# A two-block transformer kernel: the modulation's weight rows get three half-size slots of their own

## The chip, the core and the metric

One core of one Trainium2 chip runs the whole program. The metric is device time in microseconds (us) of one execution; a measurement is the median of several. A kernel is one launch, and everything it reads lies in the device's memory at the start.

## What is computed

Two model blocks over 256 tokens of width 2048, in float32, and between them a normalisation. The first block holds a state-space branch (s5), a delta-rule branch and a convolved feed-forward net of width 5632; the second holds windowed attention, an RWKV branch and a second feed-forward net. The change concerns the second block's modulation, twelve shifts, scales and gates that come from a vector `c` (and from `c_ctx`) alone:

```python
mod = jax.nn.silu(c) @ ada_w + ada_b          # ada_w: 2048 x 12288
mod_c = jax.nn.silu(c_ctx) @ ada_w + ada_b
sh1, sc1, g1, sh2, sc2, g2 = jnp.split(mod[:, None, :], 6, axis=-1)
sh1c, sc1c, g1c, sh2c, sc2c, g2c = jnp.split(mod_c, 6, axis=-1)
z = modulate(rmsnorm_2(x, norm1_g), sh1, sc1) @ w_in
zc = modulate(rmsnorm_2(xc, norm1_g), sh1c, sc1c) @ w_in
```

Nothing of it depends on the first block, so it can be computed at any time before it is used: `sh1`, `sc1` of both vectors before the second block's norms, `g1`, `sh2`, `sc2` before the attention's output is added, `g2` at the very end.

## The kernel before

**The dense layers.** Nearly all of the time goes into matrix products with large weights, written once in `dense`. It walks over a weight matrix in chunks of 256 rows by 512 columns, 928 of them. For each chunk `wchunk` loads 512 KB into a tile `w` (L233, on SyncE's queue, SP), ScalarE rounds it to fp32r into `wr` (L236), VectorE subtracts to get the rest `wl` (L237), and TensorE does 24 matmuls: weights `wr` with the high and the low part of the activations (L265, L266) and `wl` with the high part (L268). There are two slots each for `wr` and `wl` and four for `w`, and each slot is used again in turn.

**The modulation.** A matrix with one row of activations is poor work for TensorE, so VectorE does it: `ada_rows` copies a quarter of the activated vector into a PSUM tile on all partitions (`ada_c`, L197), loads weight rows of the transposed matrix, and multiplies and sums 512 columns of 128 outputs with one SCALAR_TENSOR_TENSOR and its accumulator read (L209) into a column of `part`. One such multiplication is called a step below. 512 steps are needed: 32 groups of 128 outputs for each of the two vectors (`ada_start`, 256 steps), 48 more for `c` (`ada_next`, 192 steps), and the last 16 (`ada_last`, 64 steps). A load brings two steps (512 KB, L191) into a tile `w_ada` that takes one of the same four slots as the weights' `w`, and is issued one load ahead of its use.

**What sets the order.** `ada_rows` is a generator. `dense` adds `tick_rate` after every chunk and takes one tick of the generator for each whole one (L269 to L273); the rate is 0.7, 0.3, 0.75, 0.27 and 0.25 in turn (in `program` and `ada_last`). This gives the order of the text. The order in which the five engines and the DMA queue get their instructions is then set by a scheduler that plays the program through with estimated times (`schedule_with_timeline_sim=True`): an instruction of a later place in the text can come earlier on its engine if its inputs and its slot are free. So what limits how early a step can come is, above all, when its tile's slot comes free. On the chip each engine, and SP's queue, works strictly in the order it was given.

**Places that the text speaks of.** `s5` (L879) works in eight groups, on VectorE for the most part (tiles that the profile calls s_p, s_v, s_f, s_r; each group ends with `s_y`, L928), beside the gate layers' chunks; `s5_out` splits its result into `ys5h` and `ys5l`, which the layer `glu` needs, followed by `w_out1`. `ffn1` is the first feed-forward net, whose evacuation on VectorE is a convolution (`fconv`, L1074). `rw_out` (L1519) finishes the RWKV branch head pair by head pair (tiles xr, rw_nsq, and the split `rwh`, `rwl`), which the second half of the layer `w_out2` needs. `ffn2` is the last net.

Of the kernel before, what the change touches and what calls it, by code (L numbers as in the profile page):

```python
# [10 lines left out]
F32 = mybir.dt.float32  # L11
# [3 lines left out]
ALU = mybir.AluOpType  # L15
# [61 lines left out]
class Feat:  # L77


    def __init__(self, tiles):  # L80
        self.tiles = tiles
# [8 lines left out]
class Kern:  # L90
    def __init__(self, ctx, tc, a):
        self.ctx, self.tc, self.nc, self.a = ctx, tc, tc.nc, a
        mk = lambda n, b, **k: ctx.enter_context(tc.tile_pool(name=n, bufs=b, **k))
        self.pc = mk("const", 1)
        self.pw = mk("w", 3)
        self.pb = mk("b", 1)
        self.ps = mk("ps", 1, space=PSUM)
        self.pd = mk("dr", 1, space=DRAM)
        self.n = 0
        self.ada = None  # L100
        self.N4, self.NQ, self.N2, self.NE, self.N1, self.NW, self.NWR, self.NWL = 20, 11, 8, 5, 5, 4, 2, 2


    def feat(self, n, name, dt=F32):
# [46 lines left out]
    def setup(self):  # L151
        nc, tc = self.nc, self.tc
        self.pv = self.pc.tile([128, NPV], F32, name="pv")
        nc.gpsimd.dma_start(self.pv, self.a["pv"])
        self.cst = self.pc.tile([128, NCS], F32, name="cst")
        nc.gpsimd.dma_start(self.cst, self.a["cst"])
        self.ones = self.pc.tile([128, 128], F32, name="ones")
        nc.vector.memset(self.ones, 1.0)
        self.eps = {}
        for nm, v in (("e6", EPS), ("e12", EPS * EPS), ("e6x128", 128 * EPS), ("lnx", 64e-5), ("hpi", float(np.pi / 2))):  # L160
            t = self.pc.tile([128, 1], F32, name="eps_" + nm)
            nc.vector.memset(t, v)
            self.eps[nm] = t

        th = self.t1([128, 32], name="c_th")
        o = PV["c"][0]
        cc = self.pv[:, o:o + 32]
        nc.scalar.activation(th, cc, AF.Tanh, scale=0.5)
        nc.vector.scalar_tensor_tensor(cc, th, 1.0, cc, ALU.add, ALU.mult)
        nc.vector.tensor_scalar(cc, cc, 0.5, None, ALU.mult)  # L170
        self.sil = cc
        self.part = self.pc.tile([128, 48, 4], F32, name="part")
        self.mod = self.pc.tile([128, 2, 96], F32, name="mod")


# [2 lines left out]

    def ada_next(self):
        self.ada_end()  # L180
        self.ada = self.ada_rows(0, 32, 80)

    def ada_rows(self, which, n0, n1, wide=2):

        nc = self.nc
        W = self.a["ada_wT"].rearrange("(n p) k -> p n k", p=128)
        nxt = None

        def load(q, n):
            w = self.pw.tile([128, 2, 512], F32, tag="w", name="w_ada", bufs=self.NW)  # L190
            nc.sync.dma_start(w, W[:, n:n + wide, q * 512:q * 512 + 512])  # L191
            return w
        for q in range(4):
            ps = self.ps.tile([128, 512], F32, tag="ada", name="ada_c", bufs=1)
            for j in range(4):
                k = which * 16 + q * 4 + j
                nc.tensor.matmul(ps[:, j * 128:j * 128 + 128], lhsT=self.sil[:, k:k + 1].to_broadcast([128, 128]),  # L197
                                 rhs=self.C("ident"), start=j == 0, stop=j == 3)
            for n in range(n0, n1, wide):

                if nxt is None:
                    nxt = load(q, n)
                w, nxt = nxt, None
                if n + wide < n1:
                    nxt = load(q, n + wide)
                elif q < 3:
                    nxt = load(q + 1, n0)
                for i in range(wide):
                    nc.vector.scalar_tensor_tensor(w[:, i], w[:, i], 1.0, ps, ALU.mult, ALU.mult,  # L209
                                                   accum_out=self.part[:, n - n0 + i, q:q + 1])  # L210
                yield n
        m = self.mod[:, which, n0:n1]
        nc.vector.reduce_sum(m, self.part[:, :n1 - n0], axis=mybir.AxisListType.X)
        nc.vector.tensor_tensor(m, m, self.P("ada_b")[:, n0:n1], ALU.add)
# [4 lines left out]

    def ada_last(self):  # L220
        self.ada_end()
        self.tick_rate = 0.25
        self.ada = self.ada_rows(0, 80, 96)

    def ada_tick(self):
# [50 lines left out]


    ticks = 0.0
    tick_rate = 0.7

    def split(self, hh, ll, src):

# [1469 lines left out]
    def program(self, out):  # L1752
# [5 lines left out]
        self.z_gate()  # L1758
        self.u_proj()
        self.dn_out()  # L1760
        self.tick_rate = 0.3
        self.s5_setup()
        self.s5()
        self.dn_proj()
        self.gs_gate()
        self.s5_out()
        self.tick_rate = 0.75
        self.glu()
        self.w_out1()
        self.ada_next()  # L1770
        self.tick_rate = 0.27
        self.mod1()
        self.rw_setup()
        self.ctx_path()
# [125 lines left out]
```

## Time and profile before

| | |
|---|---|
| time of three runs, median (lowest to highest) | 3565.49 us (3563.25 to 3572.38) |
| the profiled execution, its own time | 3570.66 us |
| its span, first to last instruction | 3568.9 us |
| TensorE matmul (PE), weight load (PEld) | busy 93%, 86% |
| VectorE (DVE), ScalarE (ACT), GpSimd (POOL) | busy 72%, 42%, 0% |
| mean granted TensorE clock | 0.961 of full speed |
| DMA | 635.13 MB, mean 178 GB/s |

The span is the profiled execution seen by its instructions; the time beside it has what lies around them. The trace is of one execution, so its numbers are compared with that execution's own 3570.66 us. Busy shares are means over stretches that are limited by different engines; the clock column (PEclk) is the share of full speed that TensorE was granted, and since its two levels are 1.2 and 2.4 GHz, a mean between 0.5 and 1 tells how long it was at the lower one.

### The profile page before, as it was taken

To read this page: it belongs to the slowest core of one execution; us is meant where nothing else is said; L and a number is where in the kernel's file an instruction comes from. 1 tells how busy PE (TensorE), PEld (TensorE's weight loads), DVE (VectorE), ACT (ScalarE), POOL (GpSimd) and SP (SyncE) were. 2 spreads that over 40 slices of the span, in tenths; PEclk is the share of its full clock that TensorE was granted. 3 is DMA by queue.
4 is the path that set the end of the run, shared out by engine and by line. 5 is a ranking of instruction groups with operands and counts; after the bars stand their busy time and mean duration, and the time that the engine had idled before them with its cause. 6 is when DMAs were issued, how large, how long until landed. Compare 5 with 4: busy or idle time off the path is not lost. (4 is left out here: it accounts for less than half of the span.)

```text
span 3568.9 us, 72631 instructions
## 1 busy us (share of the span) xinstructions
PE 3322.8 (93%) x30516; PEld 3086.5 (86%) x30516; DVE 2577.8 (72%) x4497; ACT 1515.1 (42%) x2148; POOL 16.9 (0%) x46
## 2 busy tenths in 40 slices
PE   7889999978999999999999998997899999999998
PEld 6778888857899898899999988886687999999998
DVE  7778899876768788866666778586765666655556
ACT  4443444424445444443344444444443443333333
POOL 0000000000000000000000000000000000000000
PEclk9889999979999999999999999998899999999999
DMA  7665566548776454456666656341022666765554
GB/s 244 205 216 183 167 182 196 181 139 277 239 224 190 135 166 154 155 175 198 211 203 217 212 181 190 111 141 63 19 92 84 200 222 230 228 195 184 183 184 142
DMA packets 342408, 635.13 MB, mean 178 GB/s; under 512 B 22112, under 2 KB 46432, under 8 KB 342080
## 3 DMA queue, kind: packets, MB, share of 16 engines
q1 hardware_dynamic: 341856, 629.42, 55.5%
q8 instruction: 239, 3.92, 0.4%
q0 software_dynamic: 224, 1.07, 0.1%
q14 instruction: 89, 0.73, 0.1%
HBM read 625.17 MB, written 4.72 MB: 176 GB/s over the span
## 5 line engine op out<-in xcount | busy, mean ns | idle before, releaser
L236 ACT CAST wr<-w 128x1024 fp32r<-128x1024 f32 (+2 forms) x928 | 953.4, 1028 | 1418.9 <-PE acc L266 1144.0
L237 DVE TENSOR_TENSOR wl<-w,wr 128x1024 fp32r<-128x1024 f32 (+2 forms) x928 | 1108.8, 1197 | 526.0 <-ACT wr L236 487.1
L265 PE MATMUL acc<-hh,wr 128*128 128x256 f32 (+2 forms) x4976 | 1266.6, 289 | 46.2 <-DVE conv L345 13.4
L266 PE MATMUL acc<-hl,wr 128*128 128x256 f32 (+2 forms) x4976 | 1260.4, 288 | 1.8 <-DVE hl L284 1.5
L265 PEld LDWEIGHTS acc<-hh,wr 128*128 128x128 f32 (+2 forms) x4976 | 970.1, 195 | 69.1 <-issue 28.1
L266 PEld LDWEIGHTS acc<-hl,wr 128*128 128x128 f32 (+2 forms) x4976 | 970.7, 195 | 14.0 <-issue 9.4
L268 PE MATMUL acc<-hh,wl 128*128 128x256 f32 (+2 forms) x4976 | 761.5, 289 | 40.3 <-DVE wl L237 39.8
L268 PEld LDWEIGHTS acc<-hh,wl 128*128 128x128 f32 (+2 forms) x4976 | 667.4, 195 | 69.1 <-DVE wl L237 50.0
L209 DVE SCALAR_TENSOR_TENSOR w_ada<-w_ada,ada_c 128x512 f32<-128x512 f32 x512 | 331.8, 683 | 216.6 <-DMA w_ada<-in_ada_wT_dram 213.0
L265 PE MATMUL acc<-hid,wr 128*128 128x256 f32 x1408 | 357.2, 287 | 4.8 <-DVE fconv L1074 3.2
L266 PE MATMUL acc<-hid,wr 128*128 128x256 f32 x1408 | 353.6, 284 | 0.0
L265 PEld LDWEIGHTS acc<-hid,wr 128*128 128x128 f32 x1408 | 271.4, 193 | 9.2 <-issue 5.0
L266 PEld LDWEIGHTS acc<-hid,wr 128*128 128x128 f32 x1408 | 271.5, 193 | 1.1 <-issue 1.0
L268 PE MATMUL acc<-hid,wl 128*128 128x256 f32 x1408 | 224.3, 286 | 4.7 <-DVE wl L237 4.6
L268 PEld LDWEIGHTS acc<-hid,wl 128*128 128x128 f32 x1408 | 191.9, 192 | 9.6 <-DVE wl L237 6.0
L1074 DVE SCALAR_TENSOR_TENSOR fconv<-acc,pv,fconv 128x255 f32<-128x255 f32 (+1 forms) x176 | 80.9, 477 | 8.8 <-ACT fconv L1072 7.6
L265 PE MATMUL acc<-ys5h,wr 128*128 128x256 f32 x256 | 66.6, 296 | 8.8 <-ACT wr L236 4.5
L265 PE MATMUL acc<-mrgh,wr 128*128 128x256 f32 x256 | 65.5, 292 | 6.0 <-ACT wr L236 5.9
L266 PE MATMUL acc<-ys5l,wr 128*128 128x256 f32 x256 | 65.7, 291 | 2.2 <-DVE ys5l L284 2.2
L1072 ACT ACTIVATE fconv<-acc,pv 128x256 f32<-128x256 f32 x88 | 40.6, 470 | 62.0 <-PE acc L268 33.2
L266 PE MATMUL acc<-mrgl,wr 128*128 128x256 f32 x256 | 64.3, 287 | 0.0
L265 PEld LDWEIGHTS acc<-ys5h,wr 128*128 128x128 f32 x256 | 50.7, 199 | 12.5 <-ACT wr L236 5.9
(532 smaller groups left out, 3679.4 us busy)
## 6 DMA issues: line engine op xcount, KB each, us to landing
w<-in_w_dram SPq DMA_DIRECT2D x264, 512.0 KB, 3.7
w<-in_w_in_dram SPq DMA_DIRECT2D x256, 512.0 KB, 4.2
w_ada<-in_ada_wT_dram SPq DMA_DIRECT2D x256, 512.0 KB, 4.3
w<-in_ffn_up_dram SPq DMA_DIRECT2D x176, 512.0 KB, 4.2
w<-in_ffn_down_dram SPq DMA_DIRECT2D x88, 512.0 KB, 4.1
w<-in_w_out_dram SPq DMA_DIRECT2D x64, 512.0 KB, 4.3
w<-in_glu_w_dram SPq DMA_DIRECT2D x32, 512.0 KB, 4.8
w<-in_dn_proj_dram SPq DMA_DIRECT2D x16, 512.0 KB, 3.7
```

Of the source, the lines that this page charges most:

```text
L209: nc.vector.scalar_tensor_tensor(w[:, i], w[:, i], 1.0, ps, ALU.mult, ALU.mult, accum_out=self.part[:, n - n0 + i, q:q + 1])
L236: nc.scalar.copy(r[:, :kb, :w], t[:, :kb, :w])
L237: nc.vector.tensor_tensor(l[:, :kb, :w], t[:, :kb, :w], r[:, :kb, :w].bitcast(F32), ALU.subtract)
L265: nc.tensor.matmul(o, lhsT=a, rhs=xh(kt), start=kt == 0 and first_j, stop=False)
L266: nc.tensor.matmul(o, lhsT=a, rhs=xl(kt), start=False, stop=False)
L268: nc.tensor.matmul(o, lhsT=a, rhs=xh(kt), start=False, stop=kt == KT - 1 and last_j)
L1072: nc.scalar.activation(t[:, j], ps[:, j], AF.Copy, scale=w(2))
L1074: v.scalar_tensor_tensor(t[:, j, k:], ps[:, j, :256 - k], w(2 - k), t[:, j, k:], ALU.mult, ALU.add)
```

## The change

The modulation's tiles get a set of slots of their own (tag `wa`): three tiles of 512 columns, 256 KB of data each, so that a load brings one step instead of two. Loads are issued two steps ahead. The weights' tag `w` goes from four slots to three, which only weights use. Since a tick is now one step, every rate is doubled; `ada_next`'s 48 groups are done as 32 and 16, so that `part` needs 32 columns instead of 48, and the tile of ones becomes one column that is read as a broadcast.

```diff
-        self.N4, self.NQ, self.N2, self.NE, self.N1, self.NW, self.NWR, self.NWL = 20, 11, 8, 5, 5, 4, 2, 2
+        self.N4, self.NQ, self.N2, self.NE, self.N1, self.NW, self.NWR, self.NWL = 20, 11, 8, 5, 5, 3, 2, 2
...
-        self.ones = self.pc.tile([128, 128], F32, name="ones")
-        nc.vector.memset(self.ones, 1.0)
+        one = self.pc.tile([128, 1], F32, name="one")
+        nc.vector.memset(one, 1.0)
+        self.ones = one.to_broadcast([128, 128])
...
-        self.part = self.pc.tile([128, 48, 4], F32, name="part")
+        self.part = self.pc.tile([128, 32, 4], F32, name="part")
...
-        self.ada = self.ada_rows(0, 32, 80)
+        self.ada = itertools.chain(self.ada_rows(0, 32, 64), self.ada_rows(0, 64, 80))
...
         def load(q, n):
-            w = self.pw.tile([128, 2, 512], F32, tag="w", name="w_ada", bufs=self.NW)
-            nc.sync.dma_start(w, W[:, n:n + wide, q * 512:q * 512 + 512])
-            return w
...
+            w = self.pw.tile([128, 512], F32, tag="wa", name="w_ada", bufs=3)
+            nc.sync.dma_start(w, W[:, n, q * 512:q * 512 + 512])
+            ahead.append(w)
+        for i, (q, n) in enumerate(steps):
...
+            for st in steps[:2] if i == 0 else []:
+                load(*st)
+            if i + 2 < len(steps):
+                load(*steps[i + 2])
+            w = ahead.pop(0)
+            nc.vector.scalar_tensor_tensor(w, w, 1.0, ps, ALU.mult, ALU.mult, accum_out=self.part[:, n - n0, q:q + 1])
+            yield n
...
-        self.tick_rate = 0.25
+        self.tick_rate = 0.5
...
-    tick_rate = 0.7
+    tick_rate = 1.4
...
-        self.tick_rate = 0.3
+        self.tick_rate = 0.6
...
-        self.tick_rate = 0.75
+        self.tick_rate = 1.5
...
-        self.tick_rate = 0.27
+        self.tick_rate = 0.54
```

How the scheduler orders the engines with it is told below for VectorE at three places. Line numbers behind `ones` differ by one or two between the two kernels. Counted over the whole order, the steps that stand on VectorE ahead of the last split of s5's result (`ys5l`) are 184 before and 328 now; from the fourth `s_y` to that split they are 26 before and 80 now. The first 448 steps are done before the 592nd of the 928 weight chunks before, and before the 272nd now; the last 64 lie between the chunks 664 and 800 before, and between 640 and 672 now. Ahead of the last split of `rw_out` stand 448 before and 499 now.

VectorE, the last group but one of s5, before (s_p, s_v, s_f and s_r are s5's tiles, s_pw its product from TensorE):

```order
L914 TENSOR_TENSOR s_p_4795<-s_pw,s_r 128x512
L915 TENSOR_TENSOR s_p_4795<-s_pw,s_f 128x512
L914 TENSOR_TENSOR s_p_4805<-s_pw,s_r 128x512
L915 TENSOR_TENSOR s_p_4805<-s_pw,s_f 128x512
L916 TENSOR_TENSOR s_p_4795<-s_p_4795 128x256
L917 TENSOR_TENSOR s_p_4795<-s_p_4795 128x256
L916 TENSOR_TENSOR s_p_4805<-s_p_4805 128x256
L917 TENSOR_TENSOR s_p_4805<-s_p_4805 128x256
L921 SCALAR_TENSOR_TENSOR s_v<-s_mag,s_p_4795 128x256 x2
L921 SCALAR_TENSOR_TENSOR s_v<-s_mag,s_p_4805 128x256 x2
```

and a group of the same kind there with the change:

```order
L912 TENSOR_TENSOR s_p_4880<-s_pw,s_r 128x512
L913 TENSOR_TENSOR s_p_4880<-s_pw,s_f 128x512
L912 TENSOR_TENSOR s_p_4890<-s_pw,s_r 128x512
L913 TENSOR_TENSOR s_p_4890<-s_pw,s_f 128x512
L208 SCALAR_TENSOR_TENSOR w_ada,part<-w_ada,ada_c 128x512
L914 TENSOR_TENSOR s_p_4880<-s_p_4880 128x256
L915 TENSOR_TENSOR s_p_4880<-s_p_4880 128x256
L208 SCALAR_TENSOR_TENSOR w_ada,part<-w_ada,ada_c 128x512 x2
L914 TENSOR_TENSOR s_p_4890<-s_p_4890 128x256
L915 TENSOR_TENSOR s_p_4890<-s_p_4890 128x256
L919 SCALAR_TENSOR_TENSOR s_v<-s_mag,s_p_4880 128x256 x2
L208 SCALAR_TENSOR_TENSOR w_ada,part<-w_ada,ada_c 128x512
```

Steps that stood far behind, in `ffn1`, now stand between s5's operations.

VectorE in `ffn1`, where the convolution of a layer's result begins, before:

```order
L237 TENSOR_TENSOR wl<-w,wr 128x1024 x4
L209 SCALAR_TENSOR_TENSOR w_ada,part<-w_ada,ada_c 128x512 x2
L1074 SCALAR_TENSOR_TENSOR fconv<-acc_18127,pv,fconv 128x255
L1074 SCALAR_TENSOR_TENSOR fconv<-acc_18127,pv,fconv 128x254
L237 TENSOR_TENSOR wl<-w,wr 128x1024
```

and the same convolution with the change:

```order
L235 TENSOR_TENSOR wl<-w,wr 128x1024 x8
L1072 SCALAR_TENSOR_TENSOR fconv<-acc_18483,pv,fconv 128x255
L1072 SCALAR_TENSOR_TENSOR fconv<-acc_18483,pv,fconv 128x254
L235 TENSOR_TENSOR wl<-w,wr 128x1024
L1072 SCALAR_TENSOR_TENSOR fconv<-acc_18484,pv,fconv 128x255
```

No step stands in `ffn1` any more.

VectorE at the end of the RWKV branch, with the change (xr is the branch's result, rw_mean, rw_rs and rw_nsq belong to its normalisation, rw_S and rw_X to the recurrence); before, the same place has no step:

```order
L1531 SCALAR_TENSOR_TENSOR xr_24059<-rw_mean,xr_24059 128x256
L208 SCALAR_TENSOR_TENSOR w_ada,part<-w_ada,ada_c 128x512 x3
L1423 TENSOR_TENSOR rw_S<-rw_S,rw_pS 128x256
L1531 SCALAR_TENSOR_TENSOR xr_24059<-rw_mean,xr_24059 128x256
L1424 TENSOR_TENSOR rw_S<-rw_S,rw_el 128x256
L208 SCALAR_TENSOR_TENSOR w_ada,part<-w_ada,ada_c 128x512 x2
L1401 TENSOR_TENSOR rw_X<-rw_px,rw_P_29141 128x256
L208 SCALAR_TENSOR_TENSOR w_ada,part<-w_ada,ada_c 128x512
L382 RECIPROCAL rw_nsq<-rw_nsq 64x256
```

The steps of `ada_last`, which stood in `ffn2`, have moved up into this place.

## Rows read from the trace of the kernel before

**Rows 1.** Busy time by stretch; columns: stretch, length, busy (count) per engine, PEclk, DMA share, GB/s.

```profile
0.00:268.00 268.00, 215.49 (x1509) 192.47 (x1510) 198.49 (x428) 112.59 (x170) 1.86 (x8) 0.89 0.71 222
268.00:606.00 338.00, 326.83 (x3020) 292.62 (x3019) 298.74 (x596) 146.81 (x182) 1.04 (x2) 0.99 0.59 181
606.00:758.00 152.00, 125.91 (x862) 100.74 (x861) 129.14 (x238) 60.17 (x76) 0.00 (x0) 0.85 0.49 149
758.00:991.00 233.00, 208.30 (x1622) 198.30 (x1621) 166.17 (x315) 92.30 (x129) 1.05 (x2) 0.97 0.76 249
991.00:1578.00 587.00, 568.23 (x6334) 527.50 (x6336) 473.29 (x853) 277.38 (x440) 5.94 (x16) 0.98 0.53 169
1578.00:2148.00 570.00, 533.44 (x4300) 519.31 (x4300) 396.97 (x631) 237.01 (x304) 1.05 (x2) 0.97 0.64 205
...
2640.00:2790.00 150.00, 133.52 (x1494) 110.46 (x1493) 87.92 (x151) 58.80 (x103) 0.00 (x0) 0.92 0.31 103
2790.00:3135.00 345.00, 345.00 (x2879) 344.92 (x2878) 220.14 (x306) 144.03 (x158) 0.00 (x0) 1.00 0.69 225
```

**Rows 2.** The same view for tile w_ada alone; a step counts two entries.

```profile
0.00:606.00 606.00, 102.75 (x316) 0.95 0.64 199
606.00:758.00 152.00, 16.84 (x52) 0.85 0.49 149
991.00:1578.00 587.00, 51.02 (x156) 0.98 0.53 169
1578.00:2148.00 570.00, 61.48 (x188) 0.97 0.64 205
```

**Rows 3.** Waits of VectorE, 0 to 758 us: total, times, longest.

```profile
DVE w_ada L209 <- DMA w_ada<-in_ada_wT_dram: 51.9, 38, 4.2
DVE wl L237 <- ACT wr L236: 21.5, 22, 5.6
```

**Rows 4.** Waits of TensorE, 606 to 758 us.

```profile
PE s_py L927 <- DVE s_p L922: 20.3, 4, 7.9
```

**Rows 5.** VectorE in order of time, 725 to 733 us: start, length, instruction, idle before.

```profile
725.89 0.68 DVE L209 SCALAR_TENSOR_TENSOR w_ada<-w_ada,ada_c 128x512 f32<-128x512 f32 x1
...
726.50 0.69 DVE L209 SCALAR_TENSOR_TENSOR w_ada<-w_ada,ada_c 128x512 f32<-128x512 f32 x1
...
731.85 0.48 DVE L928 SCALAR_TENSOR_TENSOR s_y<-s_u,pv,s_py 128x256 f32<-128x256 f32 x1 [2.51 <-PE s_py L927]
```

**Rows 6.** Waits of VectorE, 1578 to 2148 us.

```profile
DVE w_ada L209 <- DMA w_ada<-in_ada_wT_dram: 75.2, 42, 4.7
```

**Rows 7.** Waits of TensorE, 1578 to 2148 us.

```profile
PE acc L268 <- DVE wl L237: 13.6, 14, 2.3
PE acc L265 <- DVE fconv L1074: 5.0, 5, 2.7
```

**Rows 8.** VectorE in order of time, 1668 to 1690 us.

```profile
1681.55 0.69 DVE L209 SCALAR_TENSOR_TENSOR w_ada<-w_ada,ada_c 128x512 f32<-128x512 f32 x1 [2.77 <-DMA w_ada<-in_ada_wT_dram]
...
1683.69 1.22 DVE L237 TENSOR_TENSOR wl<-w,wr 128x1024 fp32r<-128x1024 f32 x1
```

**Rows 9.** TensorE in order of time, 1681 to 1686 us.

```profile
1684.96 0.75 PE L268 MATMUL acc<-hh,wl 128*128 128x256 f32 x4 [2.28 <-DVE wl L237]
```

**Rows 10.** Waits of ScalarE, 758 to 991 us.

```profile
ACT wr L236 <- DMA w<-in_w_out_dram: 36.1, 16, 4.5
...
ACT wr L236 <- DMA w<-in_glu_w_dram: 19.2, 10, 5.2
```

**Rows 11.** DMA issues: count, KB each, median us from issue to landing.

```profile
w<-in_w_dram SPq DMA_DIRECT2D x264, 512.0 KB, 3.7
...
w_ada<-in_ada_wT_dram SPq DMA_DIRECT2D x256, 512.0 KB, 4.3
...
w<-in_w_in_dram SPq DMA_DIRECT2D x16, 256.0 KB, 2.8
```

**Rows 12.** The page's costliest groups: busy us, mean ns.

```profile
L236 ACT CAST wr<-w 128x1024 fp32r<-128x1024 f32 (+2 forms) x928 | 953.4, 1028 | 1418.9 <-PE acc L266 1144.0
```

More of the change, by code (lines that the diff above doesn't have):

```diff
@@ L180, in ada_next, with ada_rows @@
         self.ada_end()
-        self.ada = self.ada_rows(0, 32, 80)
-    def ada_rows(self, which, n0, n1, wide=2):
+        self.ada = itertools.chain(self.ada_rows(0, 32, 64), self.ada_rows(0, 64, 80))
+    def ada_rows(self, which, n0, n1):
         nc = self.nc
         W = self.a["ada_wT"].rearrange("(n p) k -> p n k", p=128)
-        nxt = None
+        steps = [(q, n) for q in range(4) for n in range(n0, n1)]
+        ahead = []
         def load(q, n):
-            w = self.pw.tile([128, 2, 512], F32, tag="w", name="w_ada", bufs=self.NW)
-            nc.sync.dma_start(w, W[:, n:n + wide, q * 512:q * 512 + 512])
-            return w
[L193 to L211, printed above, removed]
@@ new lines, in load @@
+            w = self.pw.tile([128, 512], F32, tag="wa", name="w_ada", bufs=3)
+            nc.sync.dma_start(w, W[:, n, q * 512:q * 512 + 512])
+            ahead.append(w)
+        for i, (q, n) in enumerate(steps):
+            if n == n0:
+                ps = self.ps.tile([128, 512], F32, tag="ada", name="ada_c", bufs=1)
+                for j in range(4):
+                    k = which * 16 + q * 4 + j
+                    nc.tensor.matmul(ps[:, j * 128:j * 128 + 128], lhsT=self.sil[:, k:k + 1].to_broadcast([128, 128]),
+                                     rhs=self.C("ident"), start=j == 0, stop=j == 3)
+            for st in steps[:2] if i == 0 else []:
[5 more added lines that the diff above has]
+            yield n
```

## The prediction

> **What bounds the kernel now.** I read the busy time by stretch first, then the waits inside each stretch, then single instructions in order of time. Three kinds of stretch appear [rows 1]. In the second feed-forward net (2790 to 3135 us) TensorE is busy for all 345.00 us at a granted clock of 1.00: nothing but matmuls counts there. In `ffn1` (1578 to 2148) it is busy 533.44 of 570, and in the 587 us ahead of it 568.23, so there TensorE bounds with small holes. From the start to the end of s5 (758 us) neither engine is full, VectorE is busy 198.49 + 298.74 + 129.14 = 626.4 us, and in the last part of it, s5, the two hand work to and fro: TensorE waits 20.3 us for VectorE's s_p [rows 4], and VectorE 2.51 us for TensorE's s_py right behind two steps [rows 5].
>
> What do the steps cost in each? Two that stand back to back begin 0.61 us apart [rows 5]. By w_ada's entries, two a step, (316 + 52) / 2 = 184 are done by 758 us, 78 between 991 and 1578, 94 in `ffn1` [rows 2]. Their waits for a load are large: 51.9 us up to s5's end [rows 3], 75.2 us in `ffn1` [rows 6]. Most of that is idle time that nobody misses, but not all: at 1681.55 VectorE runs a step after 2.77 us of waiting, so the subtraction for the next weights comes at 1683.69 only [rows 8], and TensorE stands 2.28 us for it [rows 9].
>
> **The change, term by term.** It does not look further ahead in time: two half-size steps ahead are as much data as one load ahead before. What it changes is that a step's slot no longer waits for weights, so the scheduler lets steps run ahead. By the order, 328 steps instead of 184 stand before s5's last split, none is left in `ffn1`, and 499 instead of 448 stand before the end of `rw_out`. So work goes from stretches that TensorE bounds to stretches in which VectorE is on the path.
>
> *Start to s5's end.* 328 - 184 = 144 steps more at 0.61 us are 88 us of VectorE. The cover is its idle time there, 758 - 626.4 = 131.6 us, of which 51.9 is waiting for w_ada. These waits average 51.9 / 38 = 1.4 us. A load of 512 KB lands in 4.3 us, one of 256 KB (of another tensor) in 2.8, 1.5 less [rows 11]; that would remove most of them, and since nearly twice as many steps can now be late, I take off 37. The other 80 us is idle because VectorE waits for ScalarE's rounding (21.5 us in 22 waits [rows 3], mostly shorter than two steps) and for TensorE; a step only fits where it doesn't make the next operation late, and the order puts them inside s5's groups, where TensorE waits for VectorE. I take off 10. That leaves **+41**. Bounds: 0, if idle time takes all (131.6 is more than 88), and +88, if none does.
>
> *`glu` and `w_out1`, 758 to 991 us.* TensorE is idle 233 - 208.3 = 24.7 us [rows 1]. ScalarE waits here 36.1 and 19.2 us for weights to land [rows 10]. Weights' loads no longer wait for a slot that a step holds, nor stand in SP's queue behind one for a shared slot: **-8**, a third of TensorE's idle time. The far end is -25. The 16 steps that the order adds in this stretch are covered on VectorE (busy 166.17 of 233) but are 16 x 256 KB = 4.2 MB on the DMA engines, which at 249 GB/s is 17 us: the other end.
>
> *991 to 2148 us.* The 78 + 94 steps leave but for 24. In `ffn1` TensorE waits 13.6 us for `wl` in 14 waits, and 5.0 us for the convolution [rows 7], and the pattern of [rows 8, 9] says why: I take -10 and -2.5. Its clock there is 0.97, thus 6% of 570 = 34 us at 1.2 GHz instead of 2.4 and half of that, 17 us, lost; in the second net, where it never stops, the clock is 1.00 [rows 1]. With fewer holes I take -12. Before `ffn1`, TensorE is idle 587 - 568.23 = 18.8 us; a third, -6. Together **-30**; bounds 0 and -(13.6 + 5.0 + 17 + 18.8) = -54.
>
> *End of the RWKV branch, 2640 to 2790 us.* 499 - 448 = 51 steps more, 31 us of VectorE, which is busy 87.92 of 150 while TensorE is idle 16.5 [rows 1]. The cover is VectorE's 62 us of idle time, but the work here is a chain over both engines. A third on the path: **+10** (0 to +31). The second net, from which they come, gains nothing, since TensorE is full there.
>
> *Three slots for the weights.* In the second net a chunk takes 345.00 / (2879 / 24) = 2.87 us. Three slots go round in 8.6 us. A slot is held from issue to landing, 3.7 us [rows 11], for the rounding, 1.03 [rows 12], and for the subtraction, 1.22 [rows 8], 5.95 us in all: 2.7 spare. So **0**, hidden by those 24 matmuls a chunk; if that cover is gone, waits like those of `glu` return (ten, 19.2 us [rows 10]): upper end +19.
>
> *The rest.* 256 more load issues stand on SP, which only issues. `ada_c` is copied four more times, 16 matmuls at 0.75 / 4 = 0.19 us [rows 9], 3 us in TensorE's idle time. `ones`, `part`, one more sum: 0. But SP's queue is in order: a step that is late on VectorE holds its load's issue, and weights queued behind it are late too; this is in the upper ends.
>
> The size of a transfer is where a rule speaks against the change. The rows show 2.8 us for 256 KB against 3.7 and 4.3 for 512 KB [rows 11], so half the size costs two thirds of the time. The Trainium skill, "DMA: Bandwidth & Descriptors", section "Rules for kernel authors", asks for at least 1 MiB a DMA for the most bandwidth. Its section on the anatomy of one DMA gives some 2 us fixed for each transfer, on another issuing path; if nothing covered them, an estimate by that page is 256 x 2 = 512 us more. By rows, three slots with 2.8 us against three steps of 1.83 us is what could go wrong (a rival below).
>
> **Sum:** 41 - 8 - 30 + 10 + 0 = +13 on the profiled execution's 3570.66, 3583.7. The median of the runs stands 5.2 below that execution, so **3578 us** (+0.35%). A measurement tells 0.3%, 10.7 us, from no change.
>
> **Rivals.**
> 1. *VectorE's idle time takes the steps; faster.* Place: start to s5's end. The steps stand where the scheduler saw VectorE free, and if that is true on the chip, term one is +10, not +41. With -15 in `glu`, -45 for 991 to 2148 and +5 at `rw_out`: -45, **3520 us**. It decides if VectorE's idle time up to s5's last split falls from 131.6 to about 131.6 - 88 + 10 = 54 us. For it: 51.9 us are waits for these very loads, and idle exceeds the steps. Against: 626.4 + 88 is 714 busy of 758, more than the share of any TensorE-bound stretch, and [rows 4].
> 2. *The chain in s5 takes them whole.* Term one +88: 47 more, **3625 us**. For: [rows 4, 5]. Beside it the Trainium skill, "Perfetto Trace Analysis", section "Optimization Strategy", says that interleaving regimes with different most-contended engines may pay; steps in `ffn1` were such a mix, and this change takes it apart. Against: w_ada's waits must vanish for nothing.
> 3. *The ring of three starves VectorE.* Where steps stand more than three in a row, three take 2.8 + 0.61 = 3.4 us, not 1.83: 0.53 us more a step, 76 us over 144: 3578 + 76 = **3654 us**. Against: most stand in ones to threes.
> 4. *The order moves but the time doesn't*: gains and losses are idle time alone, or the moved waits just show elsewhere, **3565 us**. For: TensorE is busy 93% already.
>
> **How the numbers follow.** Forecast 0.44 (of it 0.23 slower by over 0.3%, since it lies just beyond, 0.17 within, 0.04 faster), first rival 0.28 (0.27 faster, 0.01 within), second 0.13, third 0.04 (slower), fourth 0.11 (0.03 faster, 0.08 within). Faster 0.34, within 0.3% 0.26, slower 0.40. The range, 3522 to 3622 us, reaches to the first rival and near the second and leaves out about half of each and the third. The forecast's own is 3560 to 3600.
>
> **What would show it.** Right: s5's last split about 30 to 40 us later than 758; VectorE's busy time up to there near 714 and its waits for w_ada near 15; `ffn1` shorter by 20 to 30 with TensorE's waits for `wl` few and the clock above 0.97; the second net still at 2.87 us a chunk and 1.00; `rw_out`'s stretch longer by some 10. Wrong: s5 ends no later than before (rival one), the weights' landing ends ScalarE's waits in the second net (three slots too few), or waits for w_ada above 51.9 (rival three).

## The result, and the profile after

The changed kernel takes 3597.26 us (median of four runs, 3594.22 to 3602.78) against 3568.47 of the kernel before beside it; the ratio is 1.0083, with a 95% interval of 1.0063 to 1.0104. It is slower, by 0.8%, where 0.35% was forecast. The profiled execution has a span of 3592.4 us against 3568.9: 23.5 us to account for, where the prediction's sum had 13.

First the busy time by stretch, cut at the same places of the program as there (columns as in [rows 1]): start to chunk 64, chunk 64 to 144, on to s5's last split, `glu` and `w_out1`, the stretch ahead of `ffn1`, `ffn1`, the end of `rw_out`, and the second net.

```profile
0.00:260.00 260.00, 204.26 (x1509) 186.01 (x1510) 204.96 (x460) 109.43 (x167) 1.86 (x8) 0.91 0.78 252
260.00:619.00 359.00, 337.73 (x3021) 299.37 (x3019) 324.08 (x693) 141.52 (x177) 1.04 (x2) 0.98 0.67 210
619.00:816.00 197.00, 140.95 (x899) 109.42 (x899) 183.92 (x399) 68.47 (x85) 0.00 (x0) 0.81 0.66 204
816.00:1042.00 226.00, 205.49 (x1627) 196.61 (x1628) 176.66 (x346) 91.40 (x129) 1.05 (x2) 0.98 0.83 275
1042.00:1632.00 590.00, 570.39 (x6392) 528.25 (x6391) 443.25 (x752) 279.62 (x440) 5.96 (x16) 0.97 0.45 145
1632.00:2160.00 528.00, 516.47 (x4233) 506.05 (x4231) 340.17 (x439) 236.77 (x302) 1.05 (x2) 0.99 0.55 174
...
2650.00:2816.00 166.00, 141.00 (x1497) 117.56 (x1496) 122.34 (x268) 58.74 (x102) 0.00 (x0) 0.89 0.55 179
2816.00:3160.00 344.00, 344.00 (x2869) 344.00 (x2869) 187.58 (x191) 145.52 (x159) 0.00 (x0) 1.00 0.58 183
```

Lay this beside [rows 1]. s5's last split comes at 816 instead of 758: 58 us lost. `glu` and `w_out1` take 226 instead of 233, the stretch ahead of `ffn1` 590 instead of 587, `ffn1` 528 instead of 570, the end of `rw_out` 166 instead of 150, the second net the same. 58 - 7 + 3 - 42 + 16 = 28, and the stretches between and after give back the other 4 or so, one or two each. Two large terms and one middling, of both signs, make a small sum.

The same view for w_ada alone (a step counts two entries) shows the steps where the order had put them: 92 in s5's second half, none in `ffn1`, 61 at the end of `rw_out`.

```profile
619.00:816.00 197.00, 61.66 (x184) 0.81 0.66 204
...
1632.00:2160.00 528.00, 0.00 (x0) 0.99 0.55 174
2650.00:2816.00 166.00, 40.87 (x122) 0.89 0.55 179
```

In s5's second half VectorE is busy 183.92 of 197 us, where it was busy 129.14 of 152: it is all but full. 66 steps more fill 44.8 us more, and the stretch is 45 us longer. Who waits for it? TensorE's waits there:

```profile
PE s_py L925 <- DVE s_p L920: 30.4, 7, 12.8
```

That is 10 us more than before [rows 4]; the rest of the 45 us isn't in this wait, for the stretch as a whole runs at VectorE's pace. The longest of these waits in order of time, on TensorE and, in the next fence, some of what VectorE did while it lasted (781.6 to 794.4 us):

```profile
794.41 1.03 PE L925 MATMUL s_py<-s_p,s_cp 128*32 128x256 f32 x2 [12.79 <-DVE s_p L920]
```

```profile
782.16 0.69 DVE L208 SCALAR_TENSOR_TENSOR w_ada<-w_ada,ada_c 128x512 f32<-128x512 f32 x1
...
783.26 0.69 DVE L208 SCALAR_TENSOR_TENSOR w_ada<-w_ada,ada_c 128x512 f32<-128x512 f32 x1 [0.41 <-DMA w_ada<-in_ada_wT_dram]
...
786.27 0.68 DVE L208 SCALAR_TENSOR_TENSOR w_ada<-w_ada,ada_c 128x512 f32<-128x512 f32 x1
786.87 0.08 DVE L208 DVE_READ_ACCUMULATOR w_ada<-w_ada,ada_c 128x1 f32 x1
786.87 0.42 DVE L914 TENSOR_TENSOR s_p<-s_p 128x256 f32<-128x256 f32 x1
...
793.58 0.69 DVE L920 TENSOR_TENSOR s_p<-s_v,s_r 128x512 f32<-128x512 f32 x1
```

Seven steps stand between the wait's start and the s_p that ends it, these three and, left out here, those at 787.54, 788.15, 790.61 and 792.99. Apart from the 0.41 us VectorE is never idle from 782.16 on, so each step pushes that s_p back by its own 0.6 us, 4.3 of the 12.79 us. The waits of VectorE for loads, from the start to 816 us, hardly fell: 43.7 us, where [rows 3] had 51.9.

```profile
DVE w_ada L208 <- DMA w_ada<-in_ada_wT_dram: 43.7, 43, 3.4
```

The page's row of load issues goes with it: half a load lands in 3.9 us, against 4.3 for a whole one [rows 11]. For the loads of the stretch up to s5's last split the medians are 3.8 and 4.2, 0.4 less, and the average wait fell by as much, from 1.37 us to 1.02, while there are 43 of them instead of 38.

```profile
w_ada<-in_ada_wT_dram SPq DMA_DIRECT2D x512, 256.0 KB, 3.9
```

In `ffn1` the gain is plain: TensorE's 13.6 us of waiting for `wl` [rows 7] are 1.0, and its waits for VectorE's convolution are gone from the list.

```profile
PE acc L266 <- DVE wl L235: 1.0, 1, 1.0
```

### The profile page after: what moved, and what is told of

The parts are those of the page before. It is cut to its first block, busy times and chain, and to the rows that moved or that the text cites. A ratio compares the mean times of both kernels' runs of the same rounds, so it can differ in the third digit from the quotient of the medians.

```text
span 3592.4 us, 73228 instructions
## 1 busy us (share of the span) xinstructions
PE 3324.7 (93%) x30548; PEld 3087.0 (86%) x30548; DVE 2583.2 (72%) x4499; ACT 1516.4 (42%) x2148; POOL 16.9 (0%) x46
## 5 line engine op out<-in xcount | busy, mean ns | idle before, releaser
L264 PEld LDWEIGHTS acc<-hl,wr 128*128 128x128 f32 (+2 forms) x4976 | 961.9, 194 | 19.5 <-issue 11.2
L208 DVE SCALAR_TENSOR_TENSOR w_ada<-w_ada,ada_c 128x512 f32<-128x512 f32 x512 | 341.4, 684 | 96.8 <-DMA w_ada<-in_ada_wT_dram 93.9
L1072 DVE SCALAR_TENSOR_TENSOR fconv<-acc,pv,fconv 128x254 f32<-128x254 f32 (+1 forms) x176 | 81.6, 478 | 16.8 <-ACT fconv L1070 15.2
L1070 ACT ACTIVATE fconv<-acc,pv 128x256 f32<-128x256 f32 x88 | 40.5, 471 | 56.2 <-PE acc L266 34.9
L263 PEld LDWEIGHTS acc<-ys5h,wr 128*128 128x128 f32 x256 | 51.6, 203 | 12.1 <-ACT ys5h L281 8.8
```

The costliest lines, as they stand in the source:

```text
L208: nc.vector.scalar_tensor_tensor(w, w, 1.0, ps, ALU.mult, ALU.mult, accum_out=self.part[:, n - n0, q:q + 1])
L263: nc.tensor.matmul(o, lhsT=a, rhs=xh(kt), start=kt == 0 and first_j, stop=False)
L264: nc.tensor.matmul(o, lhsT=a, rhs=xl(kt), start=False, stop=False)
L1070: nc.scalar.activation(t[:, j], ps[:, j], AF.Copy, scale=w(2))
L1072: v.scalar_tensor_tensor(t[:, j, k:], ps[:, j, :256 - k], w(2 - k), t[:, j, k:], ALU.mult, ALU.add)
```

## The experiments

The theory at this point: the loss is the place of the steps (VectorE's work in s5 and `rw_out`), not the slots, the size of the loads or the weights' third slot. Four rivals: half-size loads cost by themselves; three weight slots cost; s5's delay comes from the loads and not from VectorE's time; and rw_out's stretch is longer for another reason.

Most runs place steps by a hold: a step, or a quarter of them, reads a value that is rewritten from the `wl` of the weight chunk beside it in the text (times zero), so it can't run before that chunk. Loads, slots and results stay. Each table entry below is worked out from the traces: the end of the subtraction of the same weight chunk (or s5's last split) in that kernel, less that in the kernel before, in us. All are single profiled executions.

| kernel | steps by s5's last split / chunk 240 / 592 | s5's last split | chunk 240 | chunk 592 | 640 | 672 | end |
|---|---|---|---|---|---|---|---|
| before | 184 / 264 / 448 | 0 | 0 | 0 | 0 | 0 | 0 |
| the change | 328 / 424 / 448 | +58.2 | +50.7 | +9.2 | +6.9 | +26.3 | +23.5 |
| e1 quarters held | 192 / 262 / 448 | 0.0 | -22.6 | -6.3 | -2.2 | +6.9 | +12.6 |
| e2 ada_next held once | 256 / 263 / 448 | +27.5 | -4.7 | +16.6 | +19.9 | +46.1 | +43.3 |
| e3 ada_last held once | 328 / 424 / 448 | +59.5 | +57.0 | +14.2 | +15.4 | +24.5 | +31.0 |
| e4 half loads, shared slots | 184 / 262 / 448 | +25.4 | +34.6 | +69.3 | +72.1 | +68.6 | +74.8 |
| e5 all held by fours | 180 / 260 / 448 | +6.7 | -5.5 | -11.6 | -4.6 | -3.5 | -3.6 |
| e6 the first 256 free | 256 / 260 / 448 | +27.0 | -9.9 | -16.9 | -3.7 | -2.2 | -2.4 |
| e7 thin steps | 310 / 407 / 448 | -31.7 | -46.8 | -92.3 | -92.0 | -69.9 | -72.7 |
| e8 s5 spared | 148 / 260 / 448 | -11.0 | +11.6 | +12.0 | +19.1 | +19.7 | +19.5 |
| e9 two weight slots | 180 / 260 / 448 | +8.3 | +27.1 | +132.3 | +142.8 | +147.7 | +227.2 |
| e10 last 64 free | 180 / 260 / 448 | +5.8 | -4.5 | -1.6 | +11.9 | +34.5 | +31.7 |
| e11 two modulation slots | 180 / 260 / 448 | +15.9 | +26.6 | +24.8 | +21.7 | +24.1 | +24.1 |
| e12 other rates | 180 / 263 / 448 | +4.5 | -1.3 | -9.5 | -12.1 | -12.2 | -12.3 |

How far one execution can be trusted: e5 and e10 have the same order up to chunk 640 and differ by 16.5 us there, by 0.9 at s5's split. So what happens within a stretch is read from the table, and what adds up over a thousand microseconds only to some 15 us. The runs were taken in three sessions; where two of them are compared below, each is set against the kernel before that ran beside it.

### Quarters held (e1)

```diff
+        o = self.pc.tile([128, 4], F32, tag="held", name="held", bufs=2)
+        self.nc.vector.scalar_tensor_tensor(o, self.wl_now[:, 0, 0:4].bitcast(F32), 0.0,
+                                            self.sil[:, which * 16 + q * 4:which * 16 + q * 4 + 4], ALU.mult, ALU.add)
...
+                s4 = self.held(which, q) if q in hold else self.sil[:, which * 16 + q * 4:which * 16 + q * 4 + 4]
...
-                    nc.tensor.matmul(ps[:, j * 128:j * 128 + 128], lhsT=self.sil[:, k:k + 1].to_broadcast([128, 128]),
+                    nc.tensor.matmul(ps[:, j * 128:j * 128 + 128], lhsT=s4[:, j:j + 1].to_broadcast([128, 128]),
```

> The kernel of the change with its own three half-size slots and three weight slots kept, but each quarter of the steps is held back until the weight chunk that stands beside it in the text (the activated vector of that quarter is rewritten from the chunk's wl times zero). The order then has 192 steps ahead of s5's last split (before 184, change 328), 432 by the end of the first feed-forward net and none of the last 64 in rw_out. Theory (the place of the steps is the cost, not slots or load size): s5's last split within 15 us of before's 758, rw_out's stretch as before, ffn1 slow again, total 3555 to 3575 us. Rival (half-size loads or three weight slots cost by themselves): 3585 to 3600 us although the steps stand where they stood before.

Measured: 3589.14 us (ratio 1.007, 1.0048 to 1.0093). s5's last split is back to the microsecond and `glu` ends 22.6 us earlier than before, as the theory says; the total is not. The 22.6 are lost again behind chunk 240 and in the second net, just where whole bursts of 32 and 64 steps are let loose at once. The total alone would have spoken for the rival; the table spoke for bursts, and asked for a finer hold (e5).

### One part held at a time (e2, e3)

Only `ada_next`, at its first quarter (e2), or only `ada_last` (e3); the edit shown is e2's, and the hold itself is e1's:

```diff
-        self.ada = itertools.chain(self.ada_rows(0, 32, 64), self.ada_rows(0, 64, 80))
+        self.ada = itertools.chain(self.ada_rows(0, 32, 64, (0,)), self.ada_rows(0, 64, 80, ()))
```

> The change, with only the 192 steps of ada_next held back until w_out1's last chunk. 256 steps instead of 328 stand ahead of s5's last split, and the 192 come in a burst behind chunk 240, all by chunk 336. Theory: 72 steps at 0.67 us leave s5, where VectorE is full, so s5 ends some 45 us earlier than with the change; in the 409 us from chunk 240 to 336 VectorE had 329 us of work with 52 steps before and now gets 140 steps more, 94 us, so it fills up there and 20 to 40 us come back: 3570 to 3585 us. Rival (s5's delay comes from loads on the DMA engines or SP's queue, not from VectorE's work): s5 ends less than 15 us earlier, 3590 us or more.

> The change, with only the 64 steps of ada_last held back until the first weight chunk behind them in the text, so that none stands in rw_out. Theory: the stretch of rw_out gets back the 19 us that it lost with the change and the second feed-forward net, bound by TensorE, takes the 64 steps for nothing: 3575 to 3580 us. Rival (the stretch is longer because of the weights' three slots): no change, 3592 to 3600 us.

e2 measured 3609.11 us (1.0122, 1.0087 to 1.0157), slower than the change. s5 ends 30.7 us earlier, somewhat less than the 45 expected: 0.43 us for each of the 72 steps, not 0.67. But the 192 steps in one burst behind chunk 240 cost more than the 20 to 40 us allowed: by chunk 336 the kernel is 60.5 us behind before. e3 measured 3593.67 us (1.0076, 1.005 to 1.0103), where 3575 to 3580 was expected. From chunk 648 to 652, in `rw_out`, it loses 0.3 us where the change lost 12.8, so the mechanism is right; the 64 steps, released at one point, then cost 9.6 us up to chunk 672 and 8.3 up to 704. Both misses stand where a hold ends for many steps at once, so a burst is the likely cause of both; e5 tests it.

### Half loads alone (e4)

```diff
-    def ada_rows(self, which, n0, n1, wide=2):
+    def ada_rows(self, which, n0, n1, wide=1):
...
-            nc.sync.dma_start(w, W[:, n:n + wide, q * 512:q * 512 + 512])
+            nc.sync.dma_start(w[:, :wide], W[:, n:n + wide, q * 512:q * 512 + 512])
```

with all rates doubled, on the kernel before.

> The kernel before, with nothing changed but the size of the modulation's loads: one step (256 KB) a load in a slot of the shared four, all rates doubled. The order of VectorE stays that of before (184 steps ahead of s5's last split). If half-size loads cost by themselves (twice as many, each with its own latency and each taking a whole slot from the weights): 3590 us or more. If not: 3560 to 3580 us.

Measured: 3660.08 us (1.0259, 1.0217 to 1.03), 95 us above before with the same places of the steps. Half-size loads in shared slots are dear. Waits of VectorE for w_ada in the whole program, 213.0 us before, are

```profile
L209 DVE SCALAR_TENSOR_TENSOR w_ada<-w_ada,ada_c 128x512 f32<-128x512 f32 x512 | 349.0, 684 | 474.4 <-DMA w_ada<-in_ada_wT_dram 470.5
```

A load that takes a whole slot now brings one step, and the one load of look-ahead is one step instead of two. The run doesn't tell these two from the size itself. But the slots of its own are not an ornament of this change: they have to pay for the halving.

### All steps held by fours (e5): slots without the places

```diff
+        self.nc.vector.tensor_scalar(o, self.wl_now[:, 0, 0:1].bitcast(F32), 0.0, 1.0, ALU.mult, ALU.add)
...
-            nc.vector.scalar_tensor_tensor(w, w, 1.0, ps, ALU.mult, ALU.mult, accum_out=self.part[:, n - n0, q:q + 1])
+            if hold and i % hold == 0:
+                one = self.held() if self.wl_now is not None else 1.0
+            nc.vector.scalar_tensor_tensor(w, w, one if hold else 1.0, ps, ALU.mult, ALU.mult, accum_out=self.part[:, n - n0, q:q + 1])
```

> The change with its slots, loads and three weight slots, but a step may not run before the weight chunk that stands beside it in the text: every fourth step reads its factor 1.0 from a column that is rewritten from that chunk's wl times zero. VectorE's order is then that of before within a few steps (180 ahead of s5's last split, 260 at chunk 240, 435 at chunk 560, none of the last 64 in rw_out), without the bursts of 32, 64 or 192 steps of the earlier holds. Theory (the place of the steps is the cost, the slots themselves are a gain of 20 us in glu and w_out1): 3535 to 3560 us, faster than both kernels. Rival (own half-size slots or three weight slots cost by themselves): 3580 us or more.

Measured: 3567.05 us beside 3567.09 of before (ratio 0.9989, 0.9974 to 1.0003). Slots, loads and three weight slots are those of the change; only the places are those of before, and the 29 us are gone. That shows the cause of the loss. It is no faster than before, though 3535 to 3560 was expected: the slots just pay for the halving, which cost 95 us in e4. The hold brings VectorE work of its own, though (see the last section), so what the slots would gain without it isn't shown. In the trace it is 11.6 us ahead at chunk 592 and loses 7 of them up to 640, where no step stands at all (see the last section).

### The first 256 free (e6)

```diff
-        self.ada = itertools.chain(self.ada_rows(0, 0, 32), self.ada_rows(1, 0, 32))
+        self.ada = itertools.chain(self.ada_rows(0, 0, 32, 0), self.ada_rows(1, 0, 32, 0))
```

> As the run with every fourth step held, but the 256 steps of ada_start are free to run ahead as in the change; only the last 256 are held. 256 steps instead of 180 stand ahead of s5's last split. Theory: at 0.43 us a step (58 us for 136 steps and 27.5 for 64 in the first experiments) s5 ends 25 to 35 us later than with all held, some 20 of it come back in glu and w_out1, where then no step is left: 10 to 25 us slower than with all held. Rival (early steps hide in VectorE's idle time ahead of s5): no difference over 5 us.

Measured: 3570.23 us (1.0007, 0.9992 to 1.0022), 3 us above e5: neither the theory's 10 to 25 nor quite the rival. s5 does end 20.3 us later than in e5, for 76 steps, but all of it comes back in `glu` and `w_out1`, where no step is left. Its two stretches up to and behind s5's split:

```profile
0.00:785.00 785.00, 675.67 (x5411) 587.02 (x5411) 669.74 (x1405) 318.69 (x427) 2.89 (x10) 0.93 0.66 207
785.00:982.00 197.00, 193.90 (x1597) 189.56 (x1597) 121.66 (x162) 91.73 (x129) 1.05 (x2) 1.00 0.62 195
```

and in e5, with 80 steps in the second:

```profile
0.00:765.00 765.00, 673.57 (x5389) 589.31 (x5389) 640.45 (x1296) 318.54 (x426) 2.90 (x10) 0.93 0.60 186
765.00:987.00 222.00, 206.29 (x1615) 198.81 (x1616) 172.90 (x337) 93.10 (x130) 1.05 (x2) 0.96 0.81 263
```

`glu` and `w_out1` take 197 us without steps and 222 with 80, a third of a microsecond each, and a step more ahead of s5's split costs 20.3 / 76 = 0.27. So between these two places the 256 steps that have to be done ahead of chunk 240 can be shifted for next to nothing. The free ones also save 59 ns each against the held (last section), up to 15 us over the 256, so a cost of that size could hide in it. What the change added are 160 more.

### Thin steps (e7)

```diff
-            nc.vector.scalar_tensor_tensor(w, w, 1.0, ps, ALU.mult, ALU.mult, accum_out=self.part[:, n - n0, q:q + 1])
+            nc.vector.scalar_tensor_tensor(w[:, 0:8], w[:, 0:8], 1.0, ps[:, 0:8], ALU.mult, ALU.mult,
+                                           accum_out=self.part[:, n - n0, q:q + 1])
```

> The change, with each step multiplying 8 of its 512 columns, so that most of the modulation's sum is left out: the loads, slots and waits stay, VectorE's work of 0.67 us a step falls to about 0.1. 310 steps stand ahead of s5's last split, 496 ahead of the end of rw_out. Theory (s5's delay is VectorE's time for the steps): s5's last split no later than before's 758 us, total 3480 to 3545 us. Rival (the delay comes from the loads: DMA engines, SP's queue, waits of VectorE for w_ada): s5 still ends 30 us or more later than before, total 3570 us or more.

This kernel leaves out 504 of the 512 products of each step. Measured: 3498.34 us (0.9811, 0.9795 to 0.9828). s5 ends 31.7 us earlier than before, with 310 loads and their waits in place:

```profile
0.00:726.00 726.00, 662.02 (x5419) 582.59 (x5420) 549.00 (x1513) 316.19 (x425) 2.90 (x10) 0.96 0.76 243
726.00:940.00 214.00, 200.34 (x1602) 192.94 (x1602) 127.87 (x345) 89.44 (x126) 1.05 (x2) 0.98 0.87 285
```

The DMA engines carry 243 GB/s up to s5's split, more than the change's 222 over its own 816 us; so it isn't the loads that make s5 late, it is VectorE's time. Behind it, in `glu` and `w_out1`, it is the other way round: thin steps make 214 us of the change's 226, no loads and no steps at all 197 (e6). There the loads seem to count more than VectorE's time.

### Two against three slots, and the last 64 (e9, e10, e11)

All on e5: the weights' slots from three to two (e9); `ada_last` free (e10); the modulation's slots from three to two, loaded one step ahead (e11).

```diff
-        self.N4, self.NQ, self.N2, self.NE, self.N1, self.NW, self.NWR, self.NWL = 20, 11, 8, 5, 5, 3, 2, 2
+        self.N4, self.NQ, self.N2, self.NE, self.N1, self.NW, self.NWR, self.NWL = 20, 11, 8, 5, 5, 2, 2, 2
```

```diff
-        self.ada = self.ada_rows(0, 80, 96)
+        self.ada = self.ada_rows(0, 80, 96, 0)
```

```diff
-            w = self.pw.tile([128, 512], F32, tag="wa", name="w_ada", bufs=3)
+            w = self.pw.tile([128, 512], F32, tag="wa", name="w_ada", bufs=2)
...
-            for st in steps[:2] if i == 0 else []:
+            for st in steps[:1] if i == 0 else []:
...
-            if i + 2 < len(steps):
-                load(*steps[i + 2])
+            if i + 1 < len(steps):
+                load(*steps[i + 1])
```

> The run with every fourth step held, with two slots for the weights instead of three. By the prediction's sum a slot is held 5.95 us (3.7 landing, 1.03 rounding, 1.22 subtraction) and a chunk takes 2.87 us: three slots go round in 8.6 and have 2.7 to spare, two in 5.74 and lack 0.2. Theory: the second feed-forward net, full on TensorE with three slots, shows waits for weights and chunks of 3.0 us or more; 3600 us or more. Rival (the ring is never near its limit): 3560 to 3575 us.

> The run with every fourth step held, but the 64 steps of ada_last are free, so that 57 stand ahead of rw_out's last split (with the change 51) and none is left in the second net from chunk 672 on. Theory: 18 to 24 us slower than with all held, all of it between chunk 640 and 672, nothing given back in the second net: 3583 to 3593 us. Rival (the change's loss there came from the delay that it brought along, not from these steps): 3565 to 3572 us.

> The run with every fourth step held, with two instead of three slots for the modulation's tiles and loads one step ahead. Theory (places decide, the third slot only hides landing time): waits of VectorE for w_ada rise from 112 us to above 160, mostly idle time that nobody misses; 3565 to 3585 us. If the look-ahead in time is what the change's slots are worth: 3590 us or more.

e9: 3799.48 us (1.0642, 1.0626 to 1.0659). The ring's arithmetic gives the direction, not the size: in the second net, where TensorE was full at 1.00 [rows 1], it is busy 323.57 of 345 us, and from chunk 672 to the end the kernel falls back by 227.2 - 147.7 = 79.5 us, 0.31 for each of 256 chunks, so 3.2 us a chunk, where a ring of two at 5.95 us would give 2.98. The stretch, and ScalarE's longest wait in it, for weights to land:

```profile
2990.00:3335.00 345.00, 323.57 (x2523) 309.83 (x2521) 194.92 (x275) 122.67 (x131) 0.00 (x0) 0.99 0.65 199
```

```profile
ACT wr L243 <- DMA w<-in_w_dram: 188.8, 91, 4.1
```

e10: 3592.81 us (1.0052, 1.0035 to 1.0069), 21 us above the kernel before beside it (3571.96), where e5 was level with its own (the execution in the table, 3602.56, is the longest of its four). From chunk 640 to 672 it loses 22.6 us, where e5 loses 1.1, and 2.8 of them come back in the second net. That is the change's second loss, by itself: 57 steps at 0.38 us that were nearly free where they came from.

e11: 3595.26 us (1.0069, 1.0051 to 1.0087), 23 us above the kernel before beside it, beyond the 3565 to 3585 expected. VectorE's waits for w_ada rise from 112.0 to

```profile
DVE w_ada L217 <- DMA w_ada<-in_ada_wT_dram: 184.2, 148, 4.3
```

and they are not idle time that nobody misses: from s5's split to chunk 240 alone e11 goes from 9.2 us behind e5 to 32.1. So the third slot, with the second load ahead that it allows, is worth some 23 us here.

### Other rates (e8, e12)

Both on e5. e8 lowers the rate from s5 to `glu`; e12 does more steps ahead of s5 and fewer in it:

```diff
-        self.tick_rate = 0.6
         self.s5_setup()
+        self.tick_rate = 0.2
```

```diff
-    tick_rate = 1.4
+    tick_rate = 1.75
...
-        self.tick_rate = 0.6
+        self.tick_rate = 0.25
...
-        self.tick_rate = 1.5
+        self.tick_rate = 1.2
```

> As the run with every fourth step held, with the rate from s5 to glu lowered from 0.6 to 0.2 steps a chunk, so that 148 instead of 180 steps stand ahead of s5's last split and the 32 follow in glu, w_out1 and, all at once, before chunk 240 (ada_start is finished there). Theory: s5 ends 32 x 0.43 = 14 us earlier, and part of it is given back where the 32 run: 0 to 12 us faster than with all held alone. Rival (VectorE's idle time in s5 covers these few): no difference over 4 us, or slower by up to 10 for the steps in glu.

> The run with every fourth step held, with rates 1.75, 0.25 and 1.2 instead of 1.4, 0.6 and 1.5: 156 instead of 128 steps by chunk 96, 20 instead of 48 from there to chunk 172, about the same behind. Theory: s5's stretches get 28 steps less at 0.43 to 0.55 us, 12 to 15 us, and the stretches ahead 28 more at 0.25 us (8 us for 32 steps), 7 us: 4 to 10 us faster than all held, 3558 to 3565 us. Rival (a step costs the same everywhere ahead of chunk 240): 3565 to 3570 us.

e8: 3584.72 us (1.0053, 1.0037 to 1.0068), slower than e5, where 0 to 12 us faster was expected. s5 does end 17.7 us earlier than e5, 0.55 us for each of 32 steps. But `ada_start` has to be finished ahead of chunk 240, and there the last 41 steps come in a burst, at the pace of their loads: four from 961.42 to 967.02, 1.4 us each, where one takes 0.75.

```profile
961.42 0.75 DVE L217 SCALAR_TENSOR_TENSOR w_ada<-w_ada,held,ada_c 128x512 f32<-128x512 f32 x1 [0.61 <-DMA w_ada<-in_ada_wT_dram]
...
963.13 0.75 DVE L217 SCALAR_TENSOR_TENSOR w_ada<-w_ada,held,ada_c 128x512 f32<-128x512 f32 x1 [0.96 <-DMA w_ada<-in_ada_wT_dram]
...
964.03 0.75 DVE L217 SCALAR_TENSOR_TENSOR w_ada<-w_ada,held,ada_c 128x512 f32<-128x512 f32 x1
...
965.44 0.75 DVE L217 SCALAR_TENSOR_TENSOR w_ada<-w_ada,held,ada_c 128x512 f32<-128x512 f32 x1 [0.47 <-DMA w_ada<-in_ada_wT_dram]
...
967.02 0.75 DVE L217 SCALAR_TENSOR_TENSOR w_ada<-w_ada,held,ada_c 128x512 f32<-128x512 f32 x1 [0.82 <-DMA w_ada<-in_ada_wT_dram]
```

From chunk 224 to 240 it falls back by 35.5 us; the expectation's rival had the cost at 10 at most. TensorE stands nearly all of that time, at the next copy of `ada_c`, whose PSUM tile the steps are still reading:

```profile
980.80 2.05 PE L207 MATMUL ada_c<-cst,pv 128*128 128x128 f32 x8 [32.00 <-DVE w_ada L217]
```

The norms that follow need the finished sums as well (`mod`, at 980.69). So the steps run at the pace of their loads, as in the prediction's third rival, but what makes that dear is that TensorE's next work waits for the last of them.

e12: 3564.23 us beside 3571.96 (0.9984, 0.9972 to 0.9996). It is the lowest of the runs that do the whole sum, by 0.16% under the kernel before, hardly more than a measurement tells, and its interval overlaps e5's (0.9974 to 1.0003). The time is in the range expected, and the moved steps do what was expected of them up to chunk 176: ahead of chunk 96, 28 more cost 7.7 us, and from there to chunk 176, 28 fewer gain 11.8. But at chunk 240 e12 is 4.2 us behind e5, after a wait of 6.2 us for `ada_c` like e8's, and what it is ahead at the end arises between chunk 592 and 640, where neither has a step. So no gain by the moved steps is shown.

## Why the prediction came out as it did

The time goes the way that was forecast and lies in the forecast's own 3560 to 3600, but the change in time is more than twice as large: 28.8 us against 12.5. That the sum came as near as it did is partly luck. Of the terms, s5's was 17 us too low and `rw_out`'s 6, the gain from 991 to 2148 us was 9 too low, and stretches that have no term gave back 4.5: 17 + 1 - 9 + 6 - 4.5 is the 10.5 us between 13 and 23.5.

- **The step that carried it**, steps moved from stretches that TensorE bounds to stretches with VectorE on the path, is shown by e5 and e7: with the places of before the loss is gone, and without VectorE's time s5 ends early.
- **Start to s5's end**, +41 forecast, +58 measured: mis-sized. VectorE's busy time to s5's last split, forecast at 714, is 204.96 + 324.08 + 183.92 = 713.0. The idle time fell from 131.6 to 816 - 713 = 103, so 29 us of cover, not 47. What failed is the 37 us taken off the waits for w_ada: they fell by 8. Half a load landed in 3.8 us there and not in the 2.8 that [rows 11] showed for another tensor at another place, and nearly twice as many steps can be late; no run parts the two. The other idle time gave 20, where 10 was taken. The second rival (+88) was two thirds true, and the first (idle time takes all; 54 us of it left) is out. The third's sign, waits above 51.9 us, didn't come, and the fourth, that the time doesn't move, is out by the measurement.
- **`glu` and `w_out1`**, -8 forecast, -7 measured. But e6 shows that the reasoning was incomplete: without any step the stretch takes 197, 36 less than before and more than TensorE's whole idle time of 24.7; part of it is clock, 1.00 there against 0.97 [rows 1].
- **991 to 2148 us**, -30 forecast, -42 in `ffn1` and +3 ahead of it. The named wait (for `wl`, 13.6 us [rows 7]) went to 1.0 and the clock from 0.97 to 0.99. The gain of 6 ahead of `ffn1` did not come, for a reason that no run shows; that stretch still does 24 steps at its start.
- **End of the RWKV branch**, +10 forecast, +16 by stretch and +19.4 by chunks: mis-sized by the third taken; e10 shows 0.38 us a step, nearly two thirds.
- **Three weight slots**, 0 forecast: the second net keeps 344.00 / (2869 / 24) = 2.88 us a chunk and a clock of 1.00. With two slots, e9, it falls short as the ring's 5.74 against 5.95 us says, but by 0.31 us a chunk instead of 0.1.
- **The rule on transfer size**: e4 halves the loads and costs 95 us, 0.37 us for each of the 256 loads added; in it are also the halved look-ahead and the slot that each step now takes. By the estimate from the Trainium skill, "DMA: Bandwidth & Descriptors", section on the anatomy of one DMA (about 2 us fixed a transfer, given for another issuing path), it would be 512 uncovered. The direction agrees; no run here shows the fixed part by itself. The number that ought to have been weighed more is the 4.3 us in which w_ada's own loads landed, not another tensor's 2.8.
- **The rule on mixing regimes** ("Perfetto Trace Analysis", section "Optimization Strategy", of the Trainium skill) agrees with e5: steps among the matmuls of `ffn1` were such a mix, and with it restored the loss is gone, though e5 restores the places in `rw_out` too.

Price per step, worked out from the change against e5: up to chunk 240, 164 more steps cost 50.7 + 5.5 = 56.2 us, 0.34 each; from there to chunk 592, 164 fewer gain 41.5 - 6.1 = 35.4, 0.22 each (give or take 0.1, by what one execution is worth); at `rw_out` 0.38, in the second net 0.05. Against the kernel before instead of e5, whose held steps are longer, the first two are 50.7 / 160 = 0.32 and 41.5 / 160 = 0.26. So the first two differ by about the doubt on them, and the difference at `rw_out` is the plain one: the kernel is 9.2 us behind before at chunk 592, where most of s5's loss has been given back, and 19.4 more are lost from chunk 640 to 672 and not given back. The change moved steps from cheaper places to dearer ones. The net cost of the early `ada_next` alone, what is left of the 29 us beside e10's 21 and e6's 3, was not measured by itself. Why a step ahead of s5's split costs 0.27 to 0.55 (e6, e2, e8) and not its full length, and how much of the rest in `glu` is landing time and how much queue, stays open.

## What to carry to other kernels

Slots of its own for a side stream don't only take away waits; they free the scheduler to run the stream ahead, into whatever place its own times call idle. Before giving freedom, find the price of the moved work at the place where it is and at the place where it will go, and hold it (a data dependency on the neighbour's chunk will do, but a fine one: a hold that ends for 32 or 64 pieces at once makes a burst). And when half a change costs what the other half gains, as the halving and the slots did here, change one at a time.

## What the runs showed of the hardware

A load of half the size landed in 3.9 us with the change, 3.5 in e4, 4.4 in e5 and 4.5 in e7, against 4.3 for a whole one before: here its time hardly came from its size. A multiplication whose factor is read from a column instead of given as a number took longer, 744 ns against 685 in the median, so that e5 and the runs built on it carry up to 512 x 59 ns = 30 us of VectorE's time that the change has not, and 19.0 us more for 128 rewrites of that column:

```profile
L188 DVE TENSOR_SCALAR held<-wl 128x1 f32<-128x1 f32 x128 | 19.0, 149 | 1.4
```

And the attention's stretch, with the same work and no step, took 205 us at a granted clock of 0.87 before and 211 at 0.85 in e5:

```profile
2425.00:2630.00 205.00, 169.36 (x2293) 127.96 (x2293) 143.94 (x325) 89.17 (x211) 4.00 (x10) 0.87 0.10 32
```

```profile
2414.00:2625.00 211.00, 175.94 (x2295) 132.06 (x2294) 143.91 (x324) 88.91 (x211) 4.00 (x10) 0.85 0.10 31
```

What sets that clock no run here was made to show.
